# TensorE's order pinned over the main loop, a PSUM bank for the decode, five value buffers and paired state updates

## The chip, the cores and the metric

The kernel runs on one core of a Trainium2 chip. The metric is device time in microseconds (us) of one execution. The kernel before takes 2479.52 us, the median of three runs (2474.89 to 2480.68).

## The reference: what is computed

One step of a one-layer hybrid encoder. Eight heads of stick-breaking attention and eight heads of retention share one input projection and one output projection, all in float32. It is computed for a prompt (1024 frames of one new stream) and for a sample (16 new frames each of 8 running streams, so 128 rows, with 1024 cached frames behind each stream).

```python
D_MODEL, SEQ, DEC_BATCH, DEC_SEQ, PAST_LEN, HEAD_DIM, SB_HEADS, RET_HEADS = 2048, 1024, 8, 16, 1024, 128, 8, 8

h = rms_norm(x, norm_pre)
q_sb, k_sb, v_sb, gate_sb, q_r, k_r, v_r, gate_r = split(h @ w_in)      # w_in: 2048 x 8192
q_r, k_r = rope(q_r, pos), rope(k_r, pos) * HEAD_DIM ** -0.5

def stick_breaking_block(q, k, v):            # per 128 query rows, against all keys so far
    z = q @ k.T * HEAD_DIM ** -0.5
    log_keep = where(strict, log_sigmoid(-z), 0.0)                      # strict: key before query
    later = cumsum(log_keep, reverse=True) - log_keep
    return where(strict, exp(log_sigmoid(z) + later), 0.0) @ v

def retention_chunk(q, k, v, s):              # s: 128 x 128 state of a head
    o = ((q @ k.T) * intra) @ v + (q @ s) * decay_read
    s_new = s * exp(log_gamma * n) + (k * decay_write).T @ v
    return o, s_new

y = concat(head_rms_norm(o) * silu(gate)) @ w_out                       # w_out: 2048 x 2048
x = x + rms_norm(y, norm_post)
```

For the sample, the keys and values of the stick-breaking branch are the caches (`cache_sb_k`, `cache_sb_v`, 1024 frames of each of 8 streams) with the 16 new ones behind them, and the retention starts from a state given for each stream. Outputs are the new x, the new keys and values, and the new states, for prompt and sample.

## The kernel before

*Products in three parts.* Every large float32 product is split into high and low parts (`split`, L125: a copy on ScalarE, L126, and a subtraction on VectorE, L127) and done as three matmuls: high by high, high by low, low by high. In the projection by columns (`products`, L200, its matmul is L205) a 128x128 block of weights is stationary and the tokens move. In the projection by rows (`project_rows`, L228, matmul L251), which makes the values, the tokens are stationary and 256 columns of weights move, for two heads at a time. The output projection (L885 to L887) comes at the end.

*Stages.* The tokens go in two groups. The first holds prompt tiles 0 to 3 and the sample tile (640 columns, in two pieces of 256 and 384) and runs from the start to about 1207 us. The second holds prompt tiles 4 to 7 (one piece of 512) and runs to about 2042 us. The output projection takes the rest. In each group the loop over the eight heads (L799 on) issues, for a head, the projections of retention (query, key, in even heads value, gate) and then those of stick-breaking (query, key, in even heads value, gate).

*Jobs.* All other work of a head is cut into small steps, written as Python generators ("jobs"). Each product step calls `tick` (L152), which moves a clock on by one and runs one step of the first job that is due. `yield D_X` in a job means: continue that many ticks later. The constants D_X stand at L32 to L49, with one value for each token group. A tick is one L205 step of all pieces: two matmuls in the first group, one in the second; three matmuls in `project_rows`. So the constants place each step among the projection products, in the order of issue. The jobs are:

- `ret_branch` (L751): turns the retention keys by a DMA out to DRAM and four DMAs back in (`turn_out`, L431, issues at L434; `turn_in`, L437, issues at L440) and a VectorE transpose of 32x32 blocks (L761, `rkn`, scaled at L765). Then `retention` goes through the chunks, and in the first group `sample_retention` (L715) does the sample: an inner product, four products with the loaded states, and four state updates (L737, each on 32 rows), each followed by a VectorE update and a DMA out.
- `sb_branch` (L769) with `stick_breaking` (L514): for each row of query tiles scores (L534, tiles `z` in PSUM), sigmoids (ScalarE, L458), masks (GpSimd, L464), a running product (`weights`, VectorE; its last operation is L476), the same turning through DRAM, issued from GpSimd's queue, with its transpose (VectorE, L524), and at last the product with the values (L558). Each row's turn-in is issued one row later and its transpose two rows later; the last rows wait D_TR ticks after the transpose.
- `decode` (L565), first group only: cached keys come in by GpSimd's queue (L584), are transposed on VectorE (L609, `kcT`) and multiplied with the sample's queries (L600, `zc`), in four blocks. Cached values `vc` are loaded in eight parts of 512 KB by `load_v` on SyncE's queue; three loads ahead, each later one issued after the product that frees its buffer. They share the three buffers of tag `kv` with the transposed keys. Then come the scores against the new keys (L625, `zn`), sigmoids, masks and running product, and the turning (out on ScalarE's queue, in on SyncE's), the transpose L634, the product with the new values (L640) and eight products with the cached values (L647). All outputs are in one PSUM tile.

Between these steps the job yields as follows: after L625 and the weights 18 ticks (D_ROW), after the DMA out 26 (D_TO), after the turn-in 12 (D_TI), after the transpose 3 (D_TR), then 9 before each of the eight value products (D_VC).

*What sets the order.* The order of issue is not yet the order on the engines. The Tile scheduler puts the instructions of every engine, TensorE's among them, into an order of its own, and each engine then runs its list strictly in that order. Each DMA queue belongs to the engine that issues (SP, ACT, POOL). Weights come through SP with four buffers.

*PSUM.* Eight banks: two buffers each of `acc0` and `acc1` for the projections, three of tag `z` (scores, state updates, the decode's scores) and one of tag `pa` (`acc_tile`: all products with values, in prompt, decode and retention).

[...]

Of the kernel before, what the change touches and what calls it, by code (L numbers as in the profile page):

```python
# [41 lines left out]
D_VC = 9  # L42
D_RET = (9, 5)
# [12 lines left out]
def tile_hybrid_step(  # L56
# [208 lines left out]
    with ExitStack() as s1:  # L265
# [146 lines left out]
        psz = s1.enter_context(tc.tile_pool(name="psz", bufs=3, space=PSUM))  # L412
        psa = s1.enter_context(tc.tile_pool(name="psa", bufs=1, space=PSUM))

# [150 lines left out]
        def decode(h, out, qs, rest):  # L565
# [27 lines left out]
            for m in range(-KC_AHEAD, 2 * NB + 1):  # L593
                if m > 0 and m % 4 == 0:
                    s, j, _ = chunk(m - 4)
                    if j == 0:
                        z = psz.tile([P, 512], F32, name="zc", tag="z")
# [8 lines left out]
                if 0 <= m < 2 * NB:  # L606
                    if m % 2 == 0:
                        ready.append(ip.tile([P, 2, 512], F32, name="kcT", tag="kv", bufs=3))
                    nc.vector.transpose(ready[-1][:, m % 2, :], loaded.pop(0))  # L609
                    yield D_ZC  # L610
                if m + KC_AHEAD < 2 * NB:
                    loaded.append(load(m + KC_AHEAD))
            def load_v(k):
                vc = ip.tile([P, NB, P], F32, name="vc", tag="kv", bufs=3)
                nc.sync.dma_start(
                    vc, cache_v[0, :, k * P : (k + 1) * P, h, :].rearrange("b p d -> p b d")
                )
                return vc


            values = [load_v(k) for k in range(3)]
# [17 lines left out]
            po = acc_tile()  # L639
            nc.tensor.matmul(po[:, 2 * P : 3 * P], at[:, 8, :], vn[:, i, :], start=True, stop=True)  # L640

            for k in range(8):
# [7 lines left out]
                if k + 3 < 8:  # L650
                    values.append(load_v(k + 3))
# [63 lines left out]
        def sample_retention(h, out, sc, rq, rkn, rv):  # L715
            i = 4
            po = acc_tile()
            nc.tensor.matmul(po[:, 2 * P : 3 * P], sc, rv[:, i, :], start=True, stop=True)
# [6 lines left out]
            yield 2 * D_RET[phase[0]]  # L725
            for c in range(4):
# [4 lines left out]
            yield D_RET[phase[0]]  # L731
            for c in range(4):
                st = sts[c]
                r = slice(32 * c, 32 * c + 32)
                pS = psz.tile([P, 2, P], F32, name="pSs", tag="z")
                for j in range(2):
                    nc.tensor.matmul(pS[:, j, :], rkn[r, i + j, :], rv[r, i, :], start=True, stop=True)  # L737
                nc.vector.scalar_tensor_tensor(
                    st, st, math.exp(LOG_GAMMA[h] * DS), pS, ALU.mult, ALU.add
                )  # L740
                nc.scalar.dma_start(s_sample[0, 2 * c : 2 * c + 2, h].rearrange("b d e -> d b e"), st)
                yield D_RET[phase[0]]
# [6 lines left out]
            out.done(i)  # L749

# [48 lines left out]
        for gi, g in enumerate(GROUPS):  # L799
            tiles, n, nt = g["tiles"], g["n"], len(g["tiles"])  # L800
            if gi == 1:
                mov = after
            if gi:
                load_rope(gi)
            off = 0 if gi == 0 else 4
            phase[0] = gi
            for h in range(H):
                if (gi, h) == (0, 0):
                    inputs = first
                else:  # L810
                    acc = project(g, mov, col(4, h), loads, (0, 1))
                    loads = None
                    drain(ret_job)
                    inputs = ret_inputs(g, mov, h, acc)
                ret_job = Job(ret_branch(gi, g, h, *inputs), D_NAT[phase[0]])

                acc = project(g, mov, col(0, h))
                drain(sb_job)
                if gi == 1 and h == 0:
                    late.close()  # L820
                    ip = s1.enter_context(tc.tile_pool(name="ip2", bufs=1))
                q2 = [kq.tile([P, NB_TOK], F32R, name=f"q{c}", tag=f"q{c}") for c in "hl"]
                evac_split(acc, *q2)
                qs = None
                if SAMPLE in tiles:
                    qs = kq.tile([P, P], F32, name="qs", tag="qs")
                    nc.scalar.activation(qs, acc[1][0][:, 2 * P : 3 * P], AF.Copy)
                out = Out(g, "so")
                rest = {}
                sub = Job(decode(h, out, qs, rest), D_DEC) if SAMPLE in tiles else None  # L830
                acc = project(g, mov, col(1, h))
                kT = kq.tile([P, NMAX], F32, name="kT", tag="kT")
                for a, (o, m) in acc:
                    nc.scalar.activation(kT[:, o : o + m], a[:, :m], AF.Copy)
                pool, n = (ip, PT * P) if gi else (kq, NB_TOK)
                k2 = [pool.tile([P, n], F32R, name=f"k{c}", tag=f"k{c}") for c in "hl"]
                evac_split(acc, *k2, off * P)
                if gi == 1:
                    kp = wp.tile([P, NB_TOK], F32, name="kpast", tag="mr", bufs=2)
                    nc.sync.dma_start(kp, s_k[h])  # L840
                    split(k2[0][:, :NB_TOK], k2[1][:, :NB_TOK], kp)
                rest["kT"] = kT
                sb_job = Job(sb_branch(gi, g, h, out, q2, k2, kT, rest, sub), D_NAT[phase[0]])
# [221 lines left out]
```

## Time and profile before

The profiled execution took 2481.62 us; the span of its instructions is 2479.8 us.

| | |
|---|---|
| Median of three runs (lowest, highest) | 2479.52 us (2474.89, 2480.68) |
| Profiled execution; its span | 2481.62 us; 2479.8 us |
| Mean granted TensorE clock | 0.987 of full speed |
| Busy: TensorE, its weight loads, VectorE, ScalarE, GpSimd | 96%, 85%, 51%, 36%, 26% |
| TensorE busy in the first group (0 to 1207 us) | 1151.2 us |
| TensorE busy in the second group (1207 to 2042 us) | 826.2 us |
| TensorE busy in the output projection (2042 to 2479.8 us) | 410.8 us |
| DMA | 418.65 MB, mean 169 GB/s |

How to read the lines below. The page names a group of instructions by engine, operation, output <- input and line (L205 is line 205 of the kernel); PE is TensorE, PEld its weight loads, DVE is VectorE, ACT ScalarE, POOL GpSimd, SP SyncE. A name with q (SPq) is that engine's DMA queue. In the view of waits a row gives the instruction that waits, what released it, the total in us, the count and the longest. In a timeline a row begins with the time from the start of the span and the duration, both in us; what stands in brackets at its end is the idle time before it and what ended that. In the view of DMA issues the last number is the median in us from issue to landing. In the view of windows the first two numbers are the window and its length, then busy time and count of TensorE, its weight loads, VectorE, ScalarE and GpSimd; the last three are the granted TensorE clock, the DMA engines' busy share and GB/s.

### The profile page before, as it was taken

To read this page: it belongs to the slowest core of one execution; us is meant where nothing else is said; L and a number is where in the kernel's file an instruction comes from. 1 tells how busy PE (TensorE), PEld (TensorE's weight loads), DVE (VectorE), ACT (ScalarE), POOL (GpSimd) and SP (SyncE) were. 2 spreads that over 40 slices of the span, in tenths; PEclk is the share of its full clock that TensorE was granted. 3 is DMA by queue.
4 is the path that set the end of the run, shared out by engine and by line. 5 is a ranking of instruction groups with operands and counts; after the bars stand their busy time and mean duration, and the time that the engine had idled before them with its cause. 6 is when DMAs were issued, how large, how long until landed. Compare 5 with 4: busy or idle time off the path is not lost.

```text
span 2479.8 us, 40318 instructions
## 1 busy us (share of the span) xinstructions
PE 2388.2 (96%) x14832; PEld 2108.8 (85%) x14832; DVE 1252.3 (51%) x2362; ACT 903.3 (36%) x1913; POOL 641.3 (26%) x1029
## 2 busy tenths in 40 slices
PE   7999899999999999999999999999999998999998
PEld 7999888989889888998678898888889886878787
DVE  7245453445444454454645554564564455564544
ACT  6332232323223232332424434344343443444343
POOL 3244343434434343343402120120220212000000
PEclk9999999999999999999999999999999998999999
DMA  7768777696877968598875565564765557776554
GB/s 236 164 143 194 160 165 169 154 195 151 178 152 183 188 150 180 130 204 181 193 184 156 135 165 148 138 164 123 174 153 136 149 136 187 217 225 191 186 179 136
DMA packets 673094, 418.65 MB, mean 169 GB/s; under 512 B 223744, under 2 KB 617984, under 8 KB 670464
## 3 DMA queue, kind: packets, MB, share of 16 engines
q1 hardware_dynamic: 523760, 285.99, 46.8%
q0 software_dynamic: 32256, 71.36, 13.1%
q10 hardware_dynamic: 116880, 58.74, 8.6%
q8 instruction: 116, 1.90, 0.3%
q14 instruction: 82, 0.67, 0.1%
HBM read 336.24 MB, written 79.69 MB: 168 GB/s over the span
## 4 chain that ended last, share of the span: by engine, by line
PE 79%; DMA 8%; issue 7%; DVE 4%; ACT 1%; POOL 0%; SPq 0%; DVEq 0%; ACTq 0%; POOLq 0%
PE acc L205 41%; PE accn L251 15%; PE a L886 4%; PE a L887 4%; PE a L885 4%; DMA vc<-cache_sb_v 4%; PE pa L558 2%; PE zc L600 2%; PE z L534 2%; DMA mr<-s_y 1%; PE pa L647 1%; DMA mr<-s_h 1%; PE pSs L737 1%; DMA kc<-cache_sb_k 1%; DVE out L947 1%
## 5 line engine op out<-in xcount | busy, mean ns | idle before, releaser
L205 PE MATMUL acc<-ml,wh 128*128 128x256 f32 (+2 forms) x2304 | 669.5, 343 | 0.4 <-DVE ml L127 0.4
L205 PE MATMUL acc<-mh,wl 128*128 128x256 f32 (+2 forms) x2304 | 666.7, 342 | 0.2 <-DVE wl L127 0.2
L205 PE MATMUL acc<-mh,wh 128*128 128x256 f32 (+2 forms) x2304 | 664.7, 341 | 1.0 <-ACT mh L126 0.8
L127 DVE TENSOR_TENSOR wl<-wr,wh 128x512 fp32r<-128x512 f32 (+1 forms) x576 | 393.3, 690 | 499.7 <-ACT wh L126 492.9
L126 ACT ACTIVATE wh<-wr 128x512 fp32r<-128x512 f32 (+1 forms) x576 | 355.0, 625 | 689.6 <-PE acc L205 330.9
L205 PEld LDWEIGHTS acc<-mh,wl 128*128 128x128 f32 x2304 | 423.3, 189 | 50.1 <-issue 19.5
L205 PEld LDWEIGHTS acc<-mh,wh 128*128 128x128 f32 x2304 | 425.4, 190 | 44.6 <-issue 13.8
L205 PEld LDWEIGHTS acc<-ml,wh 128*128 128x128 f32 x2304 | 422.8, 190 | 40.7 <-issue 10.9
L584 POOL DMA_DIRECT2D kc<-cache_sb_k x512 | 330.7, 652 | 447.9 <-DVE kcT L609 308.8
L251 PE MATMUL accn<-whn,mh 128*128 128x256 f32 x1152 | 331.3, 288 | 0.6 <-DVE rk L288 0.6
L251 PE MATMUL accn<-wln,mh 128*128 128x256 f32 x1152 | 326.4, 284 | 1.4 <-DVE wln L127 1.3
L251 PE MATMUL accn<-whn,ml 128*128 128x256 f32 x1152 | 326.1, 283 | 0.0
L251 PEld LDWEIGHTS accn<-whn,mh 128*128 128x128 f32 x1152 | 220.7, 192 | 12.2 <-issue 10.3
L886 PE MATMUL a<-wl,mh 128*128 128x512 f32 (+1 forms) x576 | 220.8, 383 | 8.2 <-DVE wl L127 8.2
L251 PEld LDWEIGHTS accn<-wln,mh 128*128 128x128 f32 x1152 | 220.9, 192 | 5.6 <-DVE wln L127 5.0
L251 PEld LDWEIGHTS accn<-whn,ml 128*128 128x128 f32 x1152 | 220.7, 192 | 2.5 <-issue 2.5
L885 PE MATMUL a<-wh,mh 128*128 128x512 f32 (+1 forms) x576 | 219.2, 383 | 1.0 <-DVE sg L278 0.6
L887 PE MATMUL a<-wh,ml 128*128 128x512 f32 (+1 forms) x576 | 220.1, 382 | 0.0
L127 DVE TENSOR_TENSOR wln<-wrn,whn 128x512 fp32r<-128x512 f32 x128 | 87.2, 690 | 98.8 <-ACT whn L126 98.7
L886 PEld LDWEIGHTS a<-wl,mh 128*128 128x128 f32 x576 | 109.0, 189 | 31.7 <-DVE wl L127 11.2
L464 POOL TENSOR_SCALAR_AFFINE_SELECT kp<-kp 128x128 f32<-128x128 f32 x40 | 12.6, 316 | 470.9 <-ACT kp L458 470.8
L126 ACT ACTIVATE whn<-wrn 128x512 fp32r<-128x512 f32 x128 | 79.2, 634 | 149.1 <-PE accn L251 49.0
(184 smaller groups left out, 2712.4 us busy)
## 6 DMA issues: line engine op xcount, KB each, us to landing
wr<-w_in SPq DMA_DIRECT2D x384, 256.0 KB, 4.2
wr<-w_out SPq DMA_DIRECT2D x184, 256.0 KB, 3.6
wrn<-w_in SPq DMA_DIRECT2D x128, 256.0 KB, 3.2
kc<-cache_sb_k POOLq DMA_DIRECT2D x512, 64.0 KB, 4.9
vc<-cache_sb_v SPq DMA_DIRECT2D x64, 512.0 KB, 7.6
xt<-x_prompt SPq DMA_DIRECT2D x8, 1024.0 KB, 5.8
xr<-x_prompt SPq DMA_DIRECT2D x8, 1024.0 KB, 6.1
out<-out ACTq DMA_DIRECT2D x12, 512.0 KB, 2.9
```

The lines of the kernel that those rows point to most:

```text
L126: nc.scalar.activation(hi, src, AF.Copy)
L127: nc.vector.tensor_tensor(lo, src, hi.bitcast(F32), ALU.subtract)
L205: last = nc.tensor.matmul(a[:, :m], lhs[:, j, :], rhs[w][:, j, o : o + m], start=(w == 0 and j == 0 and n == 0), stop=(w == KT // WQ - 1 a ...
L251: nc.tensor.matmul(a, lhs[q][:, jj, ts], rhs[:, j, :], start=(w == 0 and j == 0 and n == 0 and t % 2 == 0), stop=(w == KT // 2 - 1 and j = ...
L534: nc.tensor.matmul(z[:, :c], q2[a][:, i * P : (i + 1) * P], k2[b][:, s : s + c], start=(m == 0), stop=(m == 2),)
L558: nc.tensor.matmul(po[:, :P], at[:, j, :], vn[:, j, :], start=(j == 0), stop=(j == t))
L584: nc.gpsimd.dma_start(kc[32 * i : 32 * i + 32, :].rearrange("p (k d) -> p k d", d=32), cache_k[0, 2 * c + j, s * 512 : (s + 1) * 512, h, 3 ...
L600: nc.tensor.matmul(z[r, :], qp[:, j, r], ready[c // 2][:, c % 2, :], start=(j == 0), stop=(j == 1))
L647: nc.tensor.matmul(po[r, : 2 * P], at[:, k, r], vc[:, 2 * c : 2 * c + 2, :], start=(k == 0), stop=(k == 7))
L885: nc.tensor.matmul(a[:, :width], hi[q][:, j, ts], wh, start=(k == 0), stop=False)
L886: nc.tensor.matmul(a[:, :width], hi[q][:, j, ts], wl, start=False, stop=False)
L887: nc.tensor.matmul(a[:, :width], lo[q][:, j, ts], wh, start=False, stop=(k == KT - 1))
```

## The change

There are six edits.

1. The main loop stands in a block that pins TensorE's order: within it TensorE runs its instructions in the order in which the program issues them. The other engines are ordered by the scheduler as before. None of the D_X constants changes.
2. PSUM is laid out anew: two banks of tag `z` instead of three, and a bank of its own (`psd`) for the decode, which takes its scores with cached keys (`zc`) and later its outputs (`po`).
3. The tag `kv` has five buffers instead of three, five value loads are issued ahead instead of three, and each later one five parts ahead.
4. In `sample_retention` the shared output bank is taken after the wait for the states, and the output is finished before the state updates.
5. The state updates go in two pairs instead of four singles. A pair alternates between two groups of 32 rows, with a bank of tag `z` for the one and the bank of tag `pa` for the other. The job has two yields of 9 ticks fewer.
[...]

```diff
--- before.py
+++ after.py
@@ -40,6 +40,7 @@
 D_ZC = 12
 D_ROW = 18
 D_VC = 9
+V_BUFS = 5
 D_RET = (9, 5)
 D_TO = (26, 23)
 D_TB = (33, 33)
@@ -409,8 +410,9 @@
         op = s1.enter_context(tc.tile_pool(name="op", bufs=2))
         late = s1.enter_context(ExitStack())
         ip = late.enter_context(tc.tile_pool(name="ip", bufs=1))
-        psz = s1.enter_context(tc.tile_pool(name="psz", bufs=3, space=PSUM))
+        psz = s1.enter_context(tc.tile_pool(name="psz", bufs=2, space=PSUM))
         psa = s1.enter_context(tc.tile_pool(name="psa", bufs=1, space=PSUM))
+        psd = s1.enter_context(tc.tile_pool(name="psd", bufs=1, space=PSUM))
 
         def store_rows(tiles, n, off, dst_p, dst_s, h):
             nc.scalar.dma_start(
@@ -594,7 +596,7 @@
                 if m > 0 and m % 4 == 0:
                     s, j, _ = chunk(m - 4)
                     if j == 0:
-                        z = psz.tile([P, 512], F32, name="zc", tag="z")
+                        z = psd.tile([P, 512], F32, name="zc", tag="pd")
                     for c in range(4):
                         r = slice(32 * c, 32 * c + 32)
                         nc.tensor.matmul(
@@ -605,20 +607,20 @@
                         sigmoids(kp, be, s * 512, z)
                 if 0 <= m < 2 * NB:
                     if m % 2 == 0:
-                        ready.append(ip.tile([P, 2, 512], F32, name="kcT", tag="kv", bufs=3))
+                        ready.append(ip.tile([P, 2, 512], F32, name="kcT", tag="kv", bufs=V_BUFS))
                     nc.vector.transpose(ready[-1][:, m % 2, :], loaded.pop(0))
                     yield D_ZC
                 if m + KC_AHEAD < 2 * NB:
                     loaded.append(load(m + KC_AHEAD))
             def load_v(k):
-                vc = ip.tile([P, NB, P], F32, name="vc", tag="kv", bufs=3)
+                vc = ip.tile([P, NB, P], F32, name="vc", tag="kv", bufs=V_BUFS)
                 nc.sync.dma_start(
                     vc, cache_v[0, :, k * P : (k + 1) * P, h, :].rearrange("b p d -> p b d")
                 )
                 return vc
 
 
-            values = [load_v(k) for k in range(3)]
+            values = [load_v(k) for k in range(V_BUFS)]
             while "kT" not in rest:
                 yield 3
             z = psz.tile([P, 512], F32, name="zn", tag="z")
@@ -636,7 +638,7 @@
             while "vn" not in rest:
                 yield 3
             vn = rest["vn"]
-            po = acc_tile()
+            po = psd.tile([P, 512], F32, name="pd", tag="pd")
             nc.tensor.matmul(po[:, 2 * P : 3 * P], at[:, 8, :], vn[:, i, :], start=True, stop=True)
 
             for k in range(8):
@@ -647,8 +649,8 @@
                     nc.tensor.matmul(
                         po[r, : 2 * P], at[:, k, r], vc[:, 2 * c : 2 * c + 2, :], start=(k == 0), stop=(k == 7)
                     )
-                if k + 3 < 8:
-                    values.append(load_v(k + 3))
+                if k + V_BUFS < 8:
+                    values.append(load_v(k + V_BUFS))
             od = out.o[:, i, :]
             nc.vector.tensor_copy(od, po[:, 2 * P : 3 * P])
             for j in range(2):
@@ -714,8 +716,6 @@
 
         def sample_retention(h, out, sc, rq, rkn, rv):
             i = 4
-            po = acc_tile()
-            nc.tensor.matmul(po[:, 2 * P : 3 * P], sc, rv[:, i, :], start=True, stop=True)
 
             sts = []
             for c in range(4):
@@ -723,23 +723,13 @@
                 nc.sync.dma_start(st, state_ret[0, 2 * c : 2 * c + 2, h].rearrange("b d e -> d b e"))
                 sts.append(st)
             yield 2 * D_RET[phase[0]]
+            po = acc_tile()
+            nc.tensor.matmul(po[:, 2 * P : 3 * P], sc, rv[:, i, :], start=True, stop=True)
             for c in range(4):
                 r = slice(32 * c, 32 * c + 32)
                 nc.tensor.matmul(
                     po[r, : 2 * P], rq[:, i * P + 32 * c : i * P + 32 * c + 32], sts[c], start=True, stop=True
                 )
-            yield D_RET[phase[0]]
-            for c in range(4):
-                st = sts[c]
-                r = slice(32 * c, 32 * c + 32)
-                pS = psz.tile([P, 2, P], F32, name="pSs", tag="z")
-                for j in range(2):
-                    nc.tensor.matmul(pS[:, j, :], rkn[r, i + j, :], rv[r, i, :], start=True, stop=True)
-                nc.vector.scalar_tensor_tensor(
-                    st, st, math.exp(LOG_GAMMA[h] * DS), pS, ALU.mult, ALU.add
-                )
-                nc.scalar.dma_start(s_sample[0, 2 * c : 2 * c + 2, h].rearrange("b d e -> d b e"), st)
-                yield D_RET[phase[0]]
             od = out.o[:, i, :]
             nc.scalar.activation(od, po[:, 2 * P : 3 * P], AF.Copy)
             for j in range(2):
@@ -747,6 +737,21 @@
                     od, po[:, j * P : (j + 1) * P], dec[:, h, 2 + j : 3 + j], od, ALU.mult, ALU.add
                 )
             out.done(i)
+            yield D_RET[phase[0]]
+
+            for c0 in (0, 2):
+                pS = [pool.tile([P, 2, P], F32, name=f"pSs{c}", tag=tag) for c, (pool, tag) in enumerate(((psz, "z"), (psa, "pa")))]
+                for j in range(2):
+                    for c in range(2):
+                        r = slice(32 * (c0 + c), 32 * (c0 + c) + 32)
+                        nc.tensor.matmul(pS[c][:, j, :], rkn[r, i + j, :], rv[r, i, :], start=True, stop=True)
+                for c in range(2):
+                    st, b = sts[c0 + c], 2 * (c0 + c)
+                    nc.vector.scalar_tensor_tensor(
+                        st, st, math.exp(LOG_GAMMA[h] * DS), pS[c], ALU.mult, ALU.add
+                    )
+                    nc.scalar.dma_start(s_sample[0, b : b + 2, h].rearrange("b d e -> d b e"), st)
+                yield D_RET[phase[0]]
 
         def ret_branch(gi, g, h, rq, rk, rv, rg):
             nt = len(g["tiles"])
@@ -796,63 +801,64 @@
         from_h = lambda k: s_h[:, k, :]
         from_y = lambda k: s_y[0][k][:, : 3 * P]
         ret_job = sb_job = loads = None
-        for gi, g in enumerate(GROUPS):
-            tiles, n, nt = g["tiles"], g["n"], len(g["tiles"])
...
+        with tc.manual_schedule(engines={mybir.EngineType.PE}):
+            for gi, g in enumerate(GROUPS):
+                tiles, n, nt = g["tiles"], g["n"], len(g["tiles"])
...
         main = after
@@ -1049,7 +1055,7 @@
     import concourse.bacc as bacc
     from concourse.bass_utils import run_bass_kernel_spmd
 
-    nc = bacc.Bacc("TRN2", target_bir_lowering=False, num_devices=1)
+    nc = bacc.Bacc("TRN2", target_bir_lowering=False, num_devices=1, dynamic_dma_scratch_size=4096)
     data = {n: np.ascontiguousarray(inputs[n]) for n in _INS}
     data.update(_constants())
     args = [
```

104 lines of the change are left out of this document (52 added, 52 removed).

## The prediction

> **What bounds the kernel now.** I read the page first, then TensorE's waits, its groups, the DMA issues, and last the timelines of one head per stage.
>
> ```profile
> span 2479.8 us, 40318 instructions
> PE 2388.2 (96%) x14832; PEld 2108.8 (85%) x14832; DVE 1252.3 (51%) x2362; ACT 903.3 (36%) x1913; POOL 641.3 (26%) x1029
> PE acc L205 41%; PE accn L251 15%; PE a L886 4%; PE a L887 4%; PE a L885 4%; DMA vc<-cache_sb_v 4%; PE pa L558 2%; PE zc L600 2%; PE z L534 2%; DMA mr<-s_y 1%; PE pa L647 1%; DMA mr<-s_h 1%; PE pSs L737 1%; DMA kc<-cache_sb_k 1%; DVE out L947 1%
> ```
>
> TensorE is busy 96% of the span, and the chain that ended last runs through its projection products (L205, L251). So a change can win only the few idle stretches of TensorE, and it loses whatever idle time it adds there. The one foreign item of size in the chain is the load of cached values, `vc`.
>
> ```profile
> PE pa L647 <- DMA vc<-cache_sb_v: 37.1, 16, 4.6
> PE pa L558 <- DVE kp L524: 7.8, 4, 2.2
> PE zc L600 <- DVE kcT L609: 2.0, 3, 1.0
> PE pa L640 <- DVE kp L634: 0.3, 2, 0.2
> ```
>
> Columns are us in total, times, longest. The decode's products with cached values (L647) wait 37.1 us for DMA. The three other places where a job's matmul reads something that a DVE transpose made, L558, L600 and L640, together wait 10.1 us. That is so because the scheduler put these matmuls behind so many projection products that their data had come. The change takes this freedom away.
>
> **The change, part by part.** The program's steps are issued by a clock of ticks, one for two matmuls in the first token group:
>
> ```profile
> 815.14 0.46 PE L205 MATMUL acc<-mh,wl 128*128 128x256 f32 x2
> 815.43 0.46 PE L205 MATMUL acc<-mh,wh 128*128 128x256 f32 x2
> 815.73 0.46 PE L205 MATMUL acc<-ml,wh 128*128 128x256 f32 x2
> ```
>
> A tick is 0.29 us. I compared TensorE's instruction order in the two programs, counting the projection products ahead of each job matmul. Most job matmuls keep their place. The ones that move forward are the ones with late data: L640 by 39 to 200 products, L647 by up to 173, the last key product of a head (L600) by up to 164, and in the second token group the last row's value product (L558) by 43 in every second head.
>
> *Five value buffers.* vc loads, and the wait they end (head 4):
>
> ```profile
> vc<-cache_sb_v SPq DMA_DIRECT2D x64, 512.0 KB, 7.6
> 824.64 1.50 PE L647 MATMUL pa<-vc,kp 128*32 128x256 f32 x24
> 831.32 0.78 PE L647 MATMUL pa<-vc,kp 128*32 128x256 f32 x8 [2.50 <-DMA vc<-cache_sb_v]
> ```
>
> Three buffers are consumed in one burst at 824.64; the fourth load, issued then, lands 7.6 us later. With five buffers the sixth load is issued after the first read and needed five steps of 9 ticks later, 45 x 0.29 = 13 us, more than 7.6. The wait goes: **-37 us**. SP carries loads four and five ahead of the decode's turn-in; 1 MB at the page's mean 169 GB/s is 6 us of transfers that run under 20 us of products. I cost that at nothing; its cover is the weight buffers, four deep, and without it 6 us a head would show.
>
> *The clock.* Each such wait is followed by slower products:
>
> ```profile
> 826.00:831.00 5.00, 2.81 (x21) 2.47 (x17) 1.38 (x3) 0.48 (x1) 0.00 (x0) 1.00 0.57 144
> 831.00:836.00 5.00, 4.68 (x25) 4.06 (x25) 0.69 (x1) 0.63 (x1) 0.00 (x0) 0.66 1.00 267
> 836.00:848.00 12.00, 12.00 (x95) 9.65 (x94) 4.99 (x11) 1.92 (x4) 4.47 (x7) 1.00 0.97 197
> ```
>
> The granted clock (third number from the end) is 0.66 in the 5 us after the 2.50 us wait, a loss of 5 x 0.34 = 1.7 us. One such per head: **-14 us**. [...]
>
> *Paired state updates.*
>
> ```profile
> L737 PE MATMUL pSs<-rv,rkn 32*128 32x128 f32 x128 | 22.6, 296 | 0.0
> 186.60 0.71 PE L737 MATMUL pSs<-rv,rkn 32*128 32x128 f32 x4
> ```
>
> Today a step multiplies on one group of 32 rows, four rows of the trace in 0.71 us, 32 steps, 22.6 us. The change alternates two groups of 32 rows with a PSUM bank each. If pairs run fully side by side half is won, 11 us; if they do not, nothing. I take **-8 us**, near the full end because no product of a pair shares rows or bank with the other. [...]
>
> *Order pinned, decode.* Here the price lies. In head 4:
>
> ```profile
> 796.72 0.49 PE L625 MATMUL zn<-kT,qs 128*128 128x128 f32 x2
> 802.27 1.35 DVE L476 TENSOR_TENSOR be<-be,kp 128x1152 f32<-128x1152 f32 x1
> 803.69 0.38 ACTq L434 DMA_DIRECT2D s_bd<-be  x1
> 820.13 0.71 DVE L524 STREAM_TRANSPOSE kb<-kb 128x512 f32<-128x512 f32 x1 [3.40 <-DMA kb<-s_be]
> 822.74 1.37 DVE L634 STREAM_TRANSPOSE kp<-be 128x1152 f32<-128x1152 f32 x1
> 824.26 0.46 PE L640 MATMUL pa<-vn,kp 128*128 128x128 f32 x2 [0.15 <-DVE kp L634]
> s_bd<-be ACTq DMA_DIRECT2D x8, 576.0 KB, 6.6
> be<-s_bd SPq DMA_DIRECT2D x32, 144.0 KB, 4.9
> ```
>
> The chain from the last score (L625) through weights, a DMA out, four DMAs in and the transpose L634 ends at 824.11. The issue order gives it 18 + 26 + 12 + 3 = 59 ticks: L640 stands 118 products behind L625, which is the product at 815.73 above. If the chain stays where it is, TensorE waits 824.1 - 815.7 = 8.4 us. If only the median DMA times bind, 803.7 + 6.6 + 4.9 + 1.4 = 816.6, a wait of 0.9 us. In head 3 the place is the first row below and the transpose is the second:
>
> ```profile
> 660.67 0.28 PE L251 MATMUL accn<-whn,mh 128*128 128x256 f32 x1
> 674.10 1.38 DVE L634 STREAM_TRANSPOSE kp<-be 128x1152 f32<-128x1152 f32 x1 [3.33 <-DMA be<-s_bd]
> 650.47 1.04 PE L600 MATMUL zc<-kcT,qp 128*32 128x512 f32 x2 [0.50 <-DVE kcT L609]
> 637.07 0.46 PE L205 MATMUL acc<-mh,wh 128*128 128x256 f32 x2
> ```
>
> That is 14.8 us, though the change also moves the key transposes (L609) forward on DVE, so part of it goes. Over eight heads I take 5 us each, the middle of 0.9 and 8.4: **+40 us**. The last key product of head 3 ran at 650.47 and now stands at 637.07, 13 us earlier; five buffers free the key transposes sooner, so I take 2 us in each of the four odd heads, **+8 us** (0 to 6 each). While L640 or L600 waits, all projection products stand behind it. DVE is in order too: L634 in head 4 sat behind L524, which waited 3.40 us.
>
> *Order pinned, second token group.*
>
> ```profile
> 1379.80 0.39 PE L205 MATMUL acc<-ml,wh 128*128 128x512 f32 x1
> 1376.26 3.12 POOL L440 DMA_DIRECT2D be<-s_be  x4 [3.95 <-DMA s_be<-be]
> 1384.78 0.71 DVE L761 STREAM_TRANSPOSE rkn<-ro 128x512 f32<-128x512 f32 x1 [0.51 <-DMA ro<-s_rk]
> 1386.70 1.24 DVE L524 STREAM_TRANSPOSE kp<-be 128x1024 f32<-128x1024 f32 x1
> 1389.55 1.95 PE L558 MATMUL pa<-vn,kp 128*128 128x128 f32 x16
> be<-s_be POOLq DMA_DIRECT2D x32, 128.0 KB, 4.7
> ```
>
> The last row's L558 ran at 1389.55; its new place is the product at 1379.80. On DVE its transpose L524 keeps its place behind L761, which waits for DMA until 1384.78, so it ends near 1387.9: 8.1 us. At the least the fourth turn-in, issued about 1378.6, lands 4.7 us later, and 1.24 us of transpose give 1384.5: 4.7 us. I take 6.5 in four heads: **+26 us**.
>
> *Clock after the new waits.* Twelve waits over 4 us, 1.7 us each: **+20 us**.
>
> *The rest.* Score tiles go from three PSUM banks to two, so a score product waits for the sigmoids of two tiles ago. No wait of that kind stands among TensorE's; between 0 and 5 us in all, taken as 0. The decode's own bank frees the shared one; that is in the moved places already. [...] The retention job ends 18 ticks earlier, beside other work: 0.
>
> Sum: -37 - 14 - 8 + 40 + 8 + 26 + 20 = **+35 us** on the profiled execution's 2481.6 us (span 2479.8 and 1.8 around), so 2517. That execution stands 2.1 us over the median of 2479.5, so I predict **2515 us**, slower by 1.4%.
>
> **Rivals.**
> *The chains fit (faster).* If out and in of the decode land in the median times, eight waits of 0.9 us are 7, the second group's 4.7 x 4 = 19, clock four times 1.7 = 7: +33 against -62 with the full pair gain, 2450 us. It decides at 815.7 - 803.7 - 1.4 = 10.6 us for the two transfers of the decode; the medians add up to 11.5. For it: the order on DVE moves the transposes of keys forward and every stall lets the other engines catch up. Against it: two engines' queues still stand before L634.
> *Everything stays late (slower still).* 8.4 x 8 = 67, 8.1 x 4 = 32, keys 6 x 4 = 24, clock 20 x 1.7 = 34, against -48 with little of the clock and pair gain: +109, 2588 us. It needs DVE held by a late turn-in in every head, as at 820.13.
> *The order hardly matters.* Most places do not move, so stalls and gains cancel within 7 us: about 2480. The moved places are just those that read late data, which speaks against it.
> [...]
>
> **How the numbers follow.** Chances: forecast 0.37, short waits free of clock 0.10, everything late 0.15, fits 0.30, cancels 0.08. About 0.3% (7 us) is what a measurement can tell from no change. Slower: 0.37 + 0.10 + 0.15 = 0.62; same 0.08; faster 0.30. The range reaches to 2442 and 2578, a little past the faster rival and short of the last; the likeliest case alone, with its bounds, is 2490 to 2560.
>
> **What would show it.** Right: TensorE's wait for `vc` near 0; waits of L640 on L634 of 20 to 65 us in 8; L558 waiting on L524 20 to 32 us more; L737 at 12 to 18 us. Wrong: L640 without waits, or a new wait for `kcT` or for a PSUM bank as the largest of TensorE's. The forecast fails on the sign if the two transfers of the decode land within 10.6 us in most heads.

## The result, and the profile after

The changed kernel takes 2602.54 us, the median of four runs (2600.12 to 2609.21), against 2478.9 us (median of four) before: a ratio of 1.0515, 95% interval 1.0493 to 1.0537. It is 5.2% slower; 1.4% was forecast, and the range ended at 2578 us.

The page of the changed kernel's profiled execution (2600.12 us):

```profile
span 2598.4 us, 40304 instructions
PE 2397.7 (92%) x14832; PEld 2129.5 (82%) x14832; DVE 1258.5 (48%) x2362; ACT 914.9 (35%) x1921; POOL 643.1 (25%) x1029
```

TensorE does the same 14832 matmuls. The span is 118.6 us longer, TensorE's busy time only 9.5 us, so 109.1 us are new idle time of TensorE. Its waits tell where (total, times, longest, in us; line numbers are now those of the changed kernel, one to twelve higher than before):

```profile
PE pa L560 <- DVE kp L526: 49.3, 11, 8.5
PE pd L642 <- DVE kp L636: 39.5, 8, 9.5
PE zc L602 <- DVE kcT L611: 36.7, 4, 12.7
PE acc L206 <- ACT vn L262: 23.0, 4, 6.9
...
PE accn L252 <- DVE rk L289: 6.6, 3, 2.2
PE acc L206 <- ACT mh L127: 5.9, 4, 2.5
```

The wait for cached values (L647 before, L649 now) is gone from this list. Three waits for VectorE's transposes, 10.1 us before, are 125.5 us. A fourth, for ScalarE to empty the banks of the value projection, was not there at all. The group of the paired state updates among TensorE's groups (busy us and mean ns of one ahead of the second bar):

```profile
L747 PE MATMUL pSs<-rv,rkn 32*128 32x128 f32 x128 | 12.4, 306 | 1.3 <-DVE ro L736 1.3
```

And one pair of it in TensorE's timeline:

```profile
488.46 0.71 PE L747 MATMUL pSs<-rv,rkn 32*128 32x128 f32 x8
```

Eight rows of the trace take the 0.71 us that four took before: 12.4 us instead of 22.6, so the pairs do run side by side.

What a wait costs behind itself is seen in the windows after the L642 of head 4, which waited 8.97 us and ran at 857.32 (the third number from the end is the granted clock):

```profile
857.00:860.00 3.00, 2.68 (x12) 2.71 (x13) 0.24 (x2) 0.00 (x0) 0.00 (x0) 0.50 0.02 5
860.00:863.00 3.00, 3.00 (x14) 3.00 (x14) 0.93 (x3) 1.03 (x3) 0.00 (x0) 0.56 0.00 0
863.00:866.00 3.00, 3.00 (x27) 2.39 (x26) 0.00 (x0) 0.00 (x0) 0.00 (x0) 1.00 0.36 100
```

That is 3 x 0.50 + 3 x 0.44 = 2.8 us of lost clock after one long wait. The mean granted clock over the execution went from 0.987 to 0.962.

### The profile page after: what moved, and what is told of

Its sections match the earlier page's. It is cut to its first block, busy times and chain, and to the rows that moved or that the text cites. A ratio compares the mean times of both kernels' runs of the same rounds, so it can differ in the third digit from the quotient of the medians.

```text
span 2598.4 us, 40304 instructions
## 1 busy us (share of the span) xinstructions
PE 2397.7 (92%) x14832; PEld 2129.5 (82%) x14832; DVE 1258.5 (48%) x2362; ACT 914.9 (35%) x1921; POOL 643.1 (25%) x1029
## 3 DMA queue, kind: packets, MB, share of 16 engines
q0 software_dynamic: 32256, 71.36, 11.8%
## 4 chain that ended last, share of the span: by engine, by line
PE 69%; DMA 12%; issue 9%; DVE 5%; POOL 2%; ACT 2%; ACTq 0%; SPq 0%; DVEq 0%; POOLq 0%
PE acc L206 37%; PE accn L252 13%; PE a L892 3%; PE a L893 3%; PE a L891 3%; DMA mr<-s_y 3%; PE pa L560 2%; DMA s_be<-kb 2%; DMA kb<-s_be 2%; PE z L536 1%; PE pd L649 1%; PE zc L602 1%; DMA out<-kn 1%; DMA mr<-s_h 1%; DMA s_be<-be 1%
## 5 line engine op out<-in xcount | busy, mean ns | idle before, releaser
L206 PE MATMUL acc<-mh,wh 128*128 128x256 f32 (+2 forms) x2304 | 670.1, 344 | 28.8 <-ACT vn L262 23.0
L206 PE MATMUL acc<-ml,wh 128*128 128x256 f32 (+2 forms) x2304 | 678.5, 348 | 0.2 <-DVE ml L128 0.2
L206 PE MATMUL acc<-mh,wl 128*128 128x256 f32 (+2 forms) x2304 | 667.9, 343 | 0.0
L206 PEld LDWEIGHTS acc<-mh,wh 128*128 128x128 f32 x2304 | 430.8, 192 | 74.2 <-ACT vn L262 23.8
L206 PEld LDWEIGHTS acc<-ml,wh 128*128 128x128 f32 x2304 | 428.1, 192 | 42.2 <-issue 13.2
L206 PEld LDWEIGHTS acc<-mh,wl 128*128 128x128 f32 x2304 | 430.3, 192 | 36.6 <-issue 8.4
L252 PE MATMUL accn<-whn,mh 128*128 128x256 f32 x1152 | 336.8, 292 | 6.6 <-DVE rk L289 6.6
L891 PEld LDWEIGHTS a<-wh,mh 128*128 128x128 f32 x576 | 109.1, 189 | 21.7 <-issue 0.6
```

The source lines that it names most:

```text
L206: last = nc.tensor.matmul(a[:, :m], lhs[:, j, :], rhs[w][:, j, o : o + m], start=(w == 0 and j == 0 and n == 0), stop=(w == KT // WQ - 1 a ...
L252: nc.tensor.matmul(a, lhs[q][:, jj, ts], rhs[:, j, :], start=(w == 0 and j == 0 and n == 0 and t % 2 == 0), stop=(w == KT // 2 - 1 and j = ...
L891: nc.tensor.matmul(a[:, :width], hi[q][:, j, ts], wh, start=(k == 0), stop=False)
```

## The experiments

Theory A, that of the prediction: the pinned order puts a few matmuls ahead of their data, and this alone costs. Theory B: resources cost (two score banks, the scratch area, five value loads in a burst). Theory C: several edits have a part in it. The scratch area is what the last added line of the diff sets, `dynamic_dma_scratch_size=4096`; the kernel before leaves it at its default.

**The order given back, and the order alone.**

```diff
 # e1, from the changed kernel
-        with tc.manual_schedule(engines={mybir.EngineType.PE}):
+        with nullcontext():
 # e2, from the changed kernel: three value buffers, single updates, default scratch
-V_BUFS = 5
+V_BUFS = 3
-    nc = bacc.Bacc("TRN2", target_bir_lowering=False, num_devices=1, dynamic_dma_scratch_size=4096)
+    nc = bacc.Bacc("TRN2", target_bir_lowering=False, num_devices=1)
...
```

> The changed kernel with the scheduler's order on TensorE given back; the other five edits stay. Theory A (places: the pinned order puts matmuls ahead of their data, and that alone costs): the waits for transposes (L560, L642, L602) fall under 15 us together, the value loads' wait stays gone, so 2479 - 37 - 14 - 10 = 2418, at most 2445 us. Theory B (resources: two score banks or the smaller scratch area slow the work): still above 2540 us. Theory C (several edits carry a part each): between 2445 and 2540 us.

> The kernel before with only the pinned order and the new PSUM layout (the pinned order needs a bank for the decode); three value buffers, single state updates, default scratch. Theory A: as slow as the changed kernel or slower, since the gains are missing, 2590 to 2650 us, with the waits for transposes at 110 to 140 us. Theory B with the scratch area as the cause: under 2530 us. Theory C: 2530 to 2590 us.

e1 took 2470.57 us, ratio to the kernel before 0.997 (0.995 to 0.9991). e2 took 2588.31 us, ratio 1.0445 (1.0412 to 1.0478). So the pinned order with its bank brings the loss by itself, and theory A holds for the sign. By their numbers both lie in the ranges of theory C, e2 at its upper end. The other four edits together made the kernel no faster under the pinned order but 0.7% slower (1.0515 against 1.0445). TensorE's waits in e1:

```profile
PE pa L560 <- DVE kp L526: 15.6, 4, 8.7
PE zc L602 <- DVE kcT L611: 13.9, 6, 4.1
...
PE pd L649 <- DMA vc<-cache_sb_v: 5.2, 4, 2.3
```

The value loads' wait fell from 37.1 to 5.2 us, but L602 and L560 wait more, and the waits for transposes are not under the 15 us expected, so that of the 61 us only 4 arrived, against the kernel before in the same session. And in e2:

```profile
PE pa L560 <- DVE kp L526: 50.4, 11, 8.1
PE pd L642 <- DVE kp L636: 49.8, 8, 13.1
PE zc L602 <- DVE kcT L611: 36.4, 8, 6.6
...
PE pd L649 <- DMA vc<-cache_sb_v: 0.4, 1, 0.4
```

With three buffers the value loads' wait is gone too. Under the pinned order the five buffers were not needed for that. What removed it there is argued, not tested by itself: nine ticks between the products give a load three steps, 27 x 0.29 = 7.8 us, and it lands in a median of 6.9 us in e2. The same three waits for transposes are there with the default scratch area and three buffers, which speaks against theory B; no run has the pinned order without the two score banks, but only 0.2 us of TensorE's waits in e2 are for one (L536 on L461).

**The layout and the scratch area alone.**

```diff
 # e11, from the kernel before: the PSUM layout alone
-        psz = s1.enter_context(tc.tile_pool(name="psz", bufs=3, space=PSUM))
+        psz = s1.enter_context(tc.tile_pool(name="psz", bufs=2, space=PSUM))
+        psd = s1.enter_context(tc.tile_pool(name="psd", bufs=1, space=PSUM))
...
 # e4, from the kernel before: the scratch area alone
-    nc = bacc.Bacc("TRN2", target_bir_lowering=False, num_devices=1)
+    nc = bacc.Bacc("TRN2", target_bir_lowering=False, num_devices=1, dynamic_dma_scratch_size=4096)
```

> The kernel before with only the new PSUM layout (two score banks, one bank for the decode), in the scheduler's order. With five buffers, pairs and this layout the scheduler's order gave 2471 us, though 37 us of waiting for values were gone. If the layout costs what the buffers won: 2490 to 2510 us. If the layout costs nothing: within 8 us of the kernel before, 2469 to 2484 us, and the gain of the buffers was eaten by waits that the new order brought.

> The kernel before with only the scratch area at 4096. Theories A and C: no change, 2479 within 8 us. Theory B with scratch as a cause: GpSimd's issues wait for room, and the key loads and row turns come later, over 2495 us.

e11: 2485.96 us, ratio 1.0034 (1.002 to 1.0048), between the two expectations: the layout costs 8 us. e4: 2478.32 us, ratio 1.0008 (0.9989 to 1.0028): nothing that can be measured.

**State updates one by one.**

```diff
 # e3, from the changed kernel: sample_retention as before
-            for c0 in (0, 2):
-                pS = [pool.tile([P, 2, P], F32, name=f"pSs{c}", tag=tag) for c, (pool, tag) in enumerate(((psz, "z"), (psa, "pa")))]
+            for c in range(4):
+                pS = psz.tile([P, 2, P], F32, name="pSs", tag="z")
...
```

> The changed kernel with the state updates one by one and the output behind them, as before (yields restored, 18 ticks longer). If the earlier state stores are what holds ScalarE before it empties the value banks: the wait of 23.0 us of L206 on ACT falls under 5 us, the updates cost 10 us more: 2602 - 23 - 8 of clock + 10 = 2580 us (2570 to 2592). If that wait comes from the pinned order itself, it stays at 20 us or more: 2605 to 2620 us.

2596.91 us, ratio 1.0482 (1.0445 to 1.0518). The wait of L206 on ScalarE is gone, as expected, but the time fell by only 5.6 us, between the two expectations and less than the two intervals can tell apart: the wait of L642, which follows it in the head, grew from 39.5 to 58.7 us. Where the 23.0 us came from is seen on ScalarE. First the kernel before, then the changed kernel, in the same head:

```profile
478.64 0.41 ACTq L741 DMA_DIRECT2D out<-st  x1
479.45 1.59 ACT L261 ACTIVATE vn<-accn 128x512 f32<-128x512 f32 x3 [1.04 <-PE accn L251]
...
486.41 0.34 ACTq L776 DMA_DIRECT2D out<-kn  x1
```

```profile
490.41 0.34 ACTq L781 DMA_DIRECT2D out<-kn  x1
...
495.17 0.50 ACTq L786 DMA_DIRECT2D out<-kn  x1
495.77 0.51 ACTq L753 DMA_DIRECT2D out<-st  x1
496.32 1.36 ACT L262 ACTIVATE vn<-accn 128x512 f32<-128x512 f32 x3 [6.21 <-DMA out<-kn]
496.97 0.90 PE L206 MATMUL acc<-mh,wh 128*128 128x256 f32 x2 [5.46 <-ACT vn L262]
```

Before, one store of a state lies ahead of the copies that empty the banks of the value projection, and the stores of keys come behind them, from 486.41. After, eight stores of keys and one of a state are issued one after the other on ScalarE's queue, from 490.41 to 496.3, and the copies stand behind them. TensorE needs these banks and waits 5.46 us. In the program the tile of the key stores, `kn`, takes the buffer of `rkn`, which the last state update reads, so that stores of keys come earlier when the updates are done earlier. In e3 they are behind the copies again, from 500.74, with the copies at 493.77.

**A shorter retention job.** The loop drains the retention job before the next head's rotary products: it lets the clock run until the job has ended. Counted in the program, in three of the four odd heads of the first group (1, 3 and 5) this is 25 ticks without a single product, while the decode's key steps, 12 ticks apart, go on being issued.

```diff
 # e5, from the changed kernel; e13, the same line in the kernel before
-D_RET = (9, 5)
+D_RET = (7, 5)
```

> The changed kernel with D_RET in the first token group at 7 ticks instead of 9 (14 yields, 28 ticks), so that the retention job of an odd head ends before the loop drains it. Theory of the drained ticks (in odd heads the clock runs 25 ticks without products while the decode's key steps go on, so the last key product comes 25 x 0.29 = 7 us too early): the waits of L602, 36.7 us in 4, fall to 15 us or less, and the time to 2570 us (2560 to 2585). Rival (the five value loads, 2.5 MB in a burst, hold up the last keys): the waits of L602 stay at 30 us or more, 2595 to 2610 us.

2554.65 us, ratio 1.0316 (1.0275 to 1.0357): 48 us less, a little more than expected. The last key product of head 3, in the changed kernel and in e5:

```profile
666.66 1.92 PE L602 MATMUL zc<-kcT,qp 128*32 128x512 f32 x2 [12.69 <-DVE kcT L611]
```

```profile
647.57 1.60 PE L602 MATMUL zc<-kcT,qp 128*32 128x512 f32 x2 [3.34 <-DVE kcT L611]
```

The waits of L602 fell from 36.7 to 10.7 us, the wait for ScalarE's copies from 23.0 us to none, and that of L642 rose from 39.5 to 55.8. In heads 1, 3 and 5 L602 waits 6.4, 9.4 and 8.0 us less, where the 25 ticks are 7 us, so the theory of the drained ticks holds for this edit. The five value loads are not needed to explain L602: e2, with three, waits 10.2, 11.4 and 10.2 us in these heads. But the drained ticks have no fixed price: with 18 more of them, in e3, these waits are 11.4, 10.9 and 12.6 us, against 9.1, 12.7 and 11.7 in the changed kernel.

What made the keys late there shows in the changed kernel on GpSimd's queue and then on VectorE, in head 3:

```profile
655.77 2.31 POOL L442 DMA_DIRECT2D kb<-s_be  x4 [4.92 <-DMA s_be<-kb]
658.07 0.65 POOL L586 DMA_DIRECT2D kc<-cache_sb_k  x1
```

```profile
665.57 0.45 DVE L526 STREAM_TRANSPOSE kb<-kb 128x256 f32<-128x256 f32 x1 [10.00 <-DMA kb<-s_be]
665.94 0.67 DVE L611 STREAM_TRANSPOSE kcT<-kc 128x512 f32<-128x512 f32 x1
```

The last part of the keys is loaded at 658.07, behind a row's turn-in that had to wait for the row's way out, and the last key transpose L611 stands behind that row's L526. Heads 1 and 5 show the same.

That ScalarE's wait went too, with the pairs kept and the job still earlier, says that it comes from the times of two groups of instructions rather than from the pairs themselves: in e5 the key stores are still ahead of the copies, but are over at 472.90, before the copies run at 476.21.

> The kernel before with only D_RET in the first group at 7 instead of 9. Theory (drained ticks cost only where the order is pinned, since the scheduler puts the key steps behind later products): within 10 us of the kernel before, 2468 to 2488 us. Rival (they cost in either order): 2430 to 2460 us.

In the kernel before the same edit gives 2472.3 us, ratio 0.9988 (0.9966 to 1.0009). So the shorter job is worth 48 us where the order is pinned (26.0 us of L602's waits and 23.0 us of ScalarE's, less 16.3 that came back at L642; the rest was not taken apart) and nothing measurable in the kernel before. For the scheduler's order with the other edits e14 below leaves this open.

**The decode's products later.**

```diff
 # e6, from the changed kernel
-D_VC = 9
+D_VC = 5
...
             nc.vector.transpose(kp[:, :n], be)
-            yield D_TR[phase[0]]
+            yield 35
```

> The changed kernel with the decode's products moved: 35 ticks instead of 3 between the transpose L636 and L642, 5 instead of 9 between the value products, so that the job ends at the same tick. Theory of places: 32 ticks are 9 us, the waits of L642, 39.5 us in 8, fall under 10 us, with at most 15 us of new waits for value loads; 2565 us (2550 to 2585). Rival (what TensorE does not wait for here it waits for at the next place, since the other engines only catch up while it stands): the sum of TensorE's waits falls by less than 10 us, over 2592 us.

2571.46 us, ratio 1.0376 (1.0347 to 1.0404). L642 does not wait any more, and the time fell by 31 us; the sum of TensorE's waits fell from 190.4 to 162.8 us. Other waits took a part; TensorE's waits in e6 have:

```profile
PE pa L560 <- DVE kb L455: 15.9, 6, 4.7
PE accn L252 <- DVE rk L289: 11.7, 3, 7.3
```

These two are 15.9 + (11.7 - 6.6) = 21 us of new waiting. So the theory of places holds, and the rival, which had the sum fall by less than 10 us, has a share.

**The last row of the second token group.** Here my reading was that L526 is late because it stands behind L766 on VectorE.

```diff
 # e7: 61; e9 and e12: 75; e12 also has the scratch area at 8192
-                ret_job = Job(ret_branch(gi, g, h, *inputs), D_NAT[phase[0]])
+                ret_job = Job(ret_branch(gi, g, h, *inputs), (14, 61)[gi])
```

> The changed kernel with the retention job of the second token group started 50 ticks later (11 us), so that its turn-in and L766 come behind the last row's L526 on VectorE. If L526 is late because it stands behind L766: the longest wait of L560 in the second group falls from 8.5 us to 5 us or less, in four heads, 14 us with the clock: 2588 us (2580 to 2594). Rival (the row's own turning through DRAM, or the small scratch area that holds its fourth issue, sets the time): the waits of L560 stay at 46 us or more, 2597 us or more.

> The changed kernel with the retention job of the second token group started 64 ticks later instead of 50 as in the run before. The programs' orders on VectorE show why the 50 ticks did nothing: the scheduler left the last row's L526 behind L766 in even heads; with 64 ticks it stands ahead of it. If the place behind L766 is the cause, the waits of L560 in even heads of the second group, 8.6, 8.3, 6.9 and 6.7 us, fall to what the row's own turn-in leaves, 3 to 5 us, and the time to 2580 to 2594 us. Rival (the turn-in alone sets it): they stay above 6 us, 2597 us or more.

> The changed kernel with the retention job of the second group 64 ticks later, as in e9, and the scratch area at 8192. If the place behind L766 and the held fourth issue of the turn-in (3.12 us there) bind side by side, so that neither alone shows: the waits of L560 in even heads of the second group fall from 6.3 to 8.9 us to 3 to 5 us, 14 us in all, 2629 - 14 = 2615 us (2605 to 2622). Rival (a further cause): they stay above 6 us, 2624 us or more.

In all three the theory missed. e7 took 2618.76 us, ratio 1.057 (1.0542 to 1.0598). VectorE in e7:

```profile
1456.64 0.71 DVE L766 STREAM_TRANSPOSE rkn<-ro 128x512 f32<-128x512 f32 x1 [6.52 <-DMA ro<-s_rk]
1457.38 0.49 DVE L770 TENSOR_SCALAR rkn<-rkn,dec 128x512 f32<-128x512 f32 x1
1457.79 1.24 DVE L526 STREAM_TRANSPOSE kp<-be 128x1024 f32<-128x1024 f32 x1
```

The scheduler had kept L526 behind L766, which was now later still, so e7 does not test the theory. In e9 (2629.18 us, ratio 1.0609, 1.058 to 1.0637) L526 stands ahead of L766, and the idle times of TensorE before L560 are still 8.7, 8.0, 8.2 and 6.1 us in the even heads; they were 8.5, 8.2, 6.8 and 6.5 in the changed kernel (the expectation counts them from start to start, which is 0.1 to 0.2 more). What L526 waits for in e9 is its own turn-in. VectorE's timeline, then GpSimd's:

```profile
1458.45 1.25 DVE L526 STREAM_TRANSPOSE kp<-be 128x1024 f32<-128x1024 f32 x1 [6.68 <-DMA be<-s_be]
```

```profile
1446.98 2.37 POOL L442 DMA_DIRECT2D be<-s_be  x3 [3.65 <-DMA s_be<-be]
1452.46 0.79 POOL L442 DMA_DIRECT2D be<-s_be  x1 [3.12 <-issue]
```

The fourth DMA of the turn-in is issued 3.12 us after the third, with no releaser in the profile. With 8192 instead of 4096 for the scratch area (e12: 2623.06 us, ratio 1.0597, 1.0553 to 1.064) all four are issued in one go (GpSimd, then VectorE):

```profile
1441.40 3.13 POOL L442 DMA_DIRECT2D be<-s_be  x4 [3.71 <-DMA s_be<-be]
```

```profile
1451.55 1.25 DVE L526 STREAM_TRANSPOSE kp<-be 128x1024 f32<-128x1024 f32 x1 [5.32 <-DMA be<-s_be]
```

So the area of 4096 is what held the fourth issue, by 3.12 us. Yet L560 still waits 7.4, 7.2, 6.4 and 6.2 us, not 3 to 5: the row's own way back from DRAM, 1451.55 - 1441.40 = 10.2 us from the first issue to the transpose, sets it once both neighbours are gone. The rivals of e9 and e12 are right by the waits; the time of e12 lies between its two ranges. Putting the retention 64 ticks later also brought new waits (L702 on L770, 13.6 us in e9 and e12), and all three kernels are slower than the changed one.

**All moves together.** e8 has the edits of e5, e6 and e7, the scratch area at 8192, and for the second group:

```diff
 # e8
-D_TR = (3, 7)
+D_TR = (3, 20)
-D_AV = (9, 11)
+D_AV = (9, 8)
 # e10: e8 with 75 for 61, eight ticks more ahead of the last L602 and 27 for 35
```

> The three moves together, the scratch area at 8192, and in the second group 20 instead of 7 ticks ahead of the last two rows' value products (taken from the yields between rows, 8 instead of 11). Theory of places: each of the three kinds of waits for a transpose falls under 12 us, and with the value loads' wait gone and the pairs faster the kernel ends ahead of the one before: 2440 to 2475 us. Rival (the waits move on to other places): over 2520 us.

> The version with all moves and the scratch area at 8192 (2517 us), with the retention of the second group started 64 ticks later, and 8 ticks more ahead of the decode's last key product, taken from those ahead of L642 (27 instead of 35). Theory of places: L560 on L526 falls from 35.4 us to under 15, L602 from 13.9 to under 8, 2517 - 20 - 6 - 8 of clock = 2483 us (2470 to 2495). Rival (waits move on to the weights and the output part): over 2500 us.

e8: 2517.1 us, ratio 1.0163 (1.0143 to 1.0182). e10: 2500.41 us, ratio 1.0097 (1.0062 to 1.0132). These moves, with the larger scratch area, gave back 102 of the 124 us, but neither reached the kernel before. e8 lies between its two expectations, e10 at the edge of the rival's: small waits appeared elsewhere. In e10 L602 is down to 2.5 us and L642 to 1.2, but L560 on L526 stays above the 15 us expected, and the rest is spread over TensorE's waits:

```profile
PE pa L560 <- DVE kp L526: 24.4, 6, 9.6
...
PE pa L560 <- DVE kb L526: 9.8, 3, 4.2
PE a L892 <- DVE wl L128: 9.1, 5, 2.9
PE pa L560 <- DVE kb L455: 8.7, 4, 3.1
PE acc L206 <- ACT wh L127: 8.0, 6, 2.2
PE pS L702 <- ACT be L461: 6.9, 6, 1.3
```

**The scheduler's order with the other edits, tuned.** e14 is e1 with D_RET at 7 and the scratch area at 8192.

> The changed kernel in the scheduler's order, with D_RET at 7 and the scratch area at 8192. Theory (drained ticks cost only where the order is pinned): within 10 us of the 2471 us of the scheduler's order, 2461 to 2481 us. Rival: 2425 to 2455 us.

2444.61 us, ratio 0.9873 (0.9825 to 0.9921): 1.3% faster than the kernel before and the fastest of all. My theory had 2461 to 2481 and missed; the time lies in the rival's range, 2425 to 2455. In the scheduler's order the two edits bring about 24 us over e1 (0.9873 against 0.997); which of them does was not separated. Alone on the kernel before, the shorter job (e13) and another size of the scratch area (e4, at 4096) changed nothing that can be measured.

## Why the prediction was wrong, step by step

The sign was right, the size was not: +35 us were forecast and 118.6 measured between the two profiled executions. The steps, in us:

| Step | Forecast | Measured | From |
|---|---|---|---|
| Wait for cached values | -37 | -37.1 | L649 waits for nothing |
| Pairs | -8 | -10.2 | 22.6 to 12.4 busy |
| Decode's L642 (L640 before) | +40 | +39.2 | 0.3 to 39.5 |
| Last key product, L602 (L600) | +8 | +34.7 | 2.0 to 36.7 |
| Last row, L560 (L558) | +26 | +40.6 | 8.7 to 49.3 |
| Retention 18 ticks earlier | 0 | +23.0 | L206 on ScalarE |
| Clock | -14 + 20 = +6 | +19.7 | busy +9.5, pairs taken out |
| Other waits | 0 | +9 | rk, mh and smaller ones |

- *Cached values and pairs*: right in size. That a pair runs side by side was the prediction's estimate; the 0.71 us for eight rows show it for these pairs. For the values the reason was wrong where the order is pinned: e2 shows that three buffers would have done there. In the scheduler's order the wait is 5.2 us in e1, with five, and 30.5 in e11, with three.
- *Decode*: right in sum, in part by luck: 5 us were taken in each of eight heads, and the waits were 4.0 to 9.5 us in five of them and 0.5 us in heads 1, 3 and 5. The test of the faster rival, 10.6 us for the two transfers, was held against the medians of single DMAs; but the four issues of the way in do not start together. In head 4 the way out is issued at 838.83 and the last issue of the way in ends at 847.44; by the trace its data land at 850.60, 11.8 us after the start, though the medians are 3.3 and 4.1 us. Five heads took 11.7 to 13.6 us, heads 1, 3 and 5 took 8.3 to 10.6. On top of that VectorE was held in its own order by a row's turn-in (ScalarE's and SyncE's queues, then VectorE):

```profile
838.83 0.38 ACTq L436 DMA_DIRECT2D s_bd<-be  x1
843.43 4.01 SPq L442 DMA_DIRECT2D be<-s_bd  x4
```

```profile
855.20 0.71 DVE L526 STREAM_TRANSPOSE kb<-kb 128x512 f32<-128x512 f32 x1 [5.35 <-DMA kb<-s_be]
855.84 1.33 DVE L636 STREAM_TRANSPOSE kp<-be 128x1152 f32<-128x1152 f32 x1
```

- *"I take 2 us in each of the four odd heads"*: this is the step that failed most. The place was right, 13 us ahead in head 3; wrong was that five buffers would free the key transposes sooner and so take most of these 13 us away. The waits were 9.1, 12.7 and 11.7 us in three odd heads and 3.1 in the first head: in head 3 nearly all of the 13 us stayed, since keys and transpose stood behind a row's turn-in. I did not see either that in these heads 25 ticks pass in the drain without any product, 25 x 0.29 = 7 us of cover that the key steps lose. e5 shows that without them most of the wait goes.
- *Last row*: in even heads the waits came to 8.5, 8.2, 6.8 and 6.5 us where 6.5 was taken and 8.1 was the upper bound: 30 us for 26. Not in the sum were 2.2 us in each of three odd heads and 5 us more for the rows that run in the output part. The reason given, L526 behind L761 (now L766), was not what set most of it: e12 shows that without it, and without the held fourth issue, 6 to 7 us stay, those of the place itself. The lower bound, 4.7 us, was too low for that: in e12 the last of the four issues ends at 1441.40 + 3.13 = 1444.53, and its data are there 7.0 us later, not the median of 4.7.
- *"The retention job ends 18 ticks earlier, beside other work: 0"*: wrong by 23 us. I named no queue that stores move past. The key stores, which wait for the last state update, went on ScalarE's queue from behind the copies that free TensorE's banks to ahead of them.
- *The rest costed at nothing*: the layout costs 8 us by e11; the scratch area nothing by e4 (2478.32 us, ratio 1.0008). At 4096 it did hold a fourth issue for 3.12 us in e9, but not as the last of the causes: at 8192, in e12, L560 still waits 6.2 to 7.4 us.
- *Clock*: the loss per long wait was 2.8 us in the windows above where 1.7 was taken, and there were more of them. The 19.7 us are an estimate, the growth of TensorE's busy time without the pairs' gain. Short waits, which the chances count as free of clock with 0.10, are not all alike: 0.66 stands behind the 2.50 us in the prediction, and in the changed kernel two waits of 2.20 us were followed by 1.00 and by 0.60 (last section).

The nearest rival, everything late at 2588 us, was right in that all three waits came, and in its condition: in all eight heads L636 runs right behind a row's L526 on VectorE. Its sum had too much for the decode (67 us), too little for L602 (24) and nothing for ScalarE's queue.

## What to carry to other kernels

Pinning TensorE's order took away the slack that the scheduler had given to late operands: here the waits for three transposes went from 10.1 to 125.5 us, and one late transpose held all products behind it, 8.97 us at the L642 of head 4. Before doing it elsewhere, count the time from each operand's start to its consumer's new place along every queue it passes, and count ticks in which nothing runs as no time at all. A wait that was removed came back in part at the next place in line (L642 from 39.5 to 58.7 us in e3 and to 55.8 in e5), so judge an edit by the sum of the waits and not by the one it aimed at.

## What the runs showed of the hardware

Two equal waits of TensorE, 2.20 us each, cost unequal clock. In two odd heads of the changed kernel L560 waited exactly as long (timeline), and the windows behind the two differ in the granted clock:

```profile
1559.72 1.16 PE L560 MATMUL pa<-vn,kp 128*128 128x128 f32 x8 [2.20 <-DVE kp L526]
1780.24 1.58 PE L560 MATMUL pa<-vn,kp 128*128 128x128 f32 x8 [2.20 <-DVE kp L526]
```

```profile
1559.70:1562.70 3.00, 2.98 (x21) 2.82 (x22) 0.20 (x1) 0.00 (x0) 0.00 (x0) 1.00 0.29 85
1780.20:1783.20 3.00, 2.96 (x13) 2.67 (x14) 0.00 (x0) 0.00 (x0) 0.00 (x0) 0.60 0.31 90
```

After the first the clock stays at 1.00, after the second it is 0.60 over 3 us, a loss of 1.2 us. So the same 2.20 us cost nothing in one place and 1.2 us in another; what sets the two apart was not shown.
